# Half rows of a DRAM-to-DRAM shift divided into strips of 10 KB and 6 KB

## The chip, the core and the metric

The kernel runs on one core of one Trainium2 chip. The metric is the device time of one execution in microseconds; the median of the runs before is 821.31 us. The profile and the trace come from one profiled execution, whose times are counted from the start of its span.

## The reference

```python
def setup_inputs():
    return {
        "x": np.random.randn(8192, 8192).astype(np.float32),
    }

def reference(x: np.ndarray) -> np.ndarray:
    return np.fft.ifftshift(x)
```

For even sizes this swaps the quadrants: out[r, c] = x[(r + 4096) % 8192, (c + 4096) % 8192]. Nothing is calculated. A row of 8192 floats is 32 KB, its left and right halves are 16 KB each, and the matrix has 268.44 MB (2^28 bytes), which have to be read once and written once.

## The kernel before, in words

All work is done by DMAs that copy straight from x to out in DRAM; no tile goes through the core. The function `copy` (L26) takes a queue, a row and a column of out, and a list of [step, count] pairs, works out where the same elements lie in x, and issues one DMA at L29. Two queues issue: `nc.sync` (SP; q1 in the profile) copies the left halves of out, `nc.scalar` (ACT; q10) the right halves.

A block is `rows` = 16 x 16 = 256 rows. The DMA of a block's half has the pattern `back`: 16 rows beside each other, 16 steps back by 16 rows each, and in each of them 4096 floats that lie together. The innermost run of 16 KB is one packet of a DMA engine. The outermost count of 16 is dealt to the 16 DMA engines, one row of every 16 to each; an engine then walks backward through the block with a step of 16 rows (512 KB) from packet to packet. One such DMA moves 4 MB.

The loop takes groups of four blocks from the last rows of out to the first, and in each the blocks 3, 2, 1, 0 on SP; on ACT, block (n + 2) % 4 of the same group goes with block n on SP, so that the two queues are two blocks (512 rows) apart.

Ahead of the loop ACT issues seven small copies. They move the last 16 rows of the right half of one block in four strips of 4 KB, three of which are divided by rows into 14 + 2, 9 + 7 and 4 + 12. A DMA whose outermost count is k below 16 uses k engines, so the engines get between one and seven of these 64 pieces. The DMA that moves the rest of this block, with the pattern `rest`, is one step of 16 rows shorter.

In all there are 32 DMAs on SP and 39 on ACT. The framework has eight semaphores for DMAs and gives them out in turn, so that a DMA that gets a semaphore already given has to wait at its issue until the DMA that had it before is done. In steady state four DMAs of each queue are in flight, and each issue waits for the DMA four back on its own queue. Within a DMA engine both queues have a row of packets waiting, and the engine takes from one and the other.

Of the kernel before, what the change touches and what calls it, by code (L numbers as in the profile page):

```python
# [1 line left out]

# [4 lines left out]


ENGINES = 16


@with_exitstack
def kernel(
    ctx: ExitStack,
    tc: tile.TileContext,
    x: bass.AP,
    out: bass.AP,
):
    nc = tc.nc
    R, C = x.shape  # L20
    hr = R // 2
    hc = C // 2
    per = 16
    rows = ENGINES * per

    def copy(queue, row, col, dims):  # L26

        src = (row + hr) % R * C + (col + hc) % C
        queue.dma_start(  # L29
            out=bass.AP(out.tensor, out.offset + row * C + col, dims),  # L30
            in_=bass.AP(x.tensor, x.offset + src, dims),
        )

    start = R - 3 * rows
    strip = hc // 4
    for n, k in enumerate((14, 9, 4)):
        col = hc + n * strip
        copy(nc.scalar, start + rows - ENGINES, col, [[C, k], [1, strip]])  # L40
        copy(nc.scalar, start + rows - ENGINES + k, col, [[C, ENGINES - k], [1, strip]])
    copy(nc.scalar, start + rows - ENGINES, hc + 3 * strip, [[C, ENGINES], [1, strip]])


    back = [[C, ENGINES], [-ENGINES * C, per], [1, hc]]
    rest = [[C, ENGINES], [-ENGINES * C, per - 1], [1, hc]]
    for first in range(R - 4 * rows, -1, -4 * rows):
        for n in (3, 2, 1, 0):
            copy(nc.sync, first + n * rows + rows - ENGINES, 0, back)
            right = first + (n + 2) % 4 * rows  # L50
            if right == start:
                copy(nc.scalar, right + rows - 2 * ENGINES, hc, rest)
            else:
                copy(nc.scalar, right + rows - ENGINES, hc, back)


# [1 line left out]
_INS = ['x']  # L58
_OUTS = [((8192, 8192), 'float32')]


# [23 lines left out]
```

## Time and profile before

| | |
|---|---|
| median of 3 runs | 821.31 us (820.95 to 821.79) |
| span of the profiled execution (its time as a whole is not given beside it) | 810.9 us |
| what the median has over the span | 10.4 us |
| data moved, mean rate over the span | 268.44 MB, 331 GB/s |
| HBM read and written together | 662 GB/s |
| DMA issues of 4 MB: SP / ACT | 32 / 31, and one of 3840 KB on ACT |
| from issue to landing, median and longest | 100.8 us, 104.6 us |
| one DMA instruction on SP | 571 ns |
| last issue on SP / ACT | at 706.2 us / 714.7 us |

How to read it: the engines of the core are all but idle, so the usual rows of busy engines and of the critical chain hold nothing here (the chain is 0.4 us of start-up on POOL). The rows that matter are those of the DMA engines: their busy share and their rate by slice of time, the packets and the share of each queue, and the durations of single packets in the trace. A busy DMA engine is not one at its full pace; a packet that waits for memory counts as busy.

### The profile page before, as it was taken

Reading aid. Unit: us, or ns where it says so; the run is one execution under the profiler, and the core shown is the slowest. Engines: PE = TensorE matmul, PEld = TensorE weight load, DVE = VectorE, ACT = ScalarE, POOL = GpSimd, SP = SyncE. Lnnn points to the kernel's source line nnn. Section 1 sums busy time; section 2 is a strip of 40 time slices with the busy share of each in tenths; the row PEclk is TensorE's granted clock in tenths of the full one; section 3 lists DMA queues with packets and bytes.
Section 4 is the critical chain, followed back from the end, with each engine's and each line's share of the span. In section 5 each row is a group of like instructions: output and inputs, shape, how many; then the busy total and the mean of one; then the engine's idle time right before and its main releaser. Section 6 shows DMA issues by size and latency. Waiting matters only on the chain. (4 is left out here: it accounts for less than half of the span.)

```text
span 810.9 us, 116 instructions
## 1 busy us (share of the span) xinstructions
POOL 0.2 (0%) x4
## 2 busy tenths in 40 slices
POOL 0000000000000000000000000000000000000000
DMA  9999999999999999999999999999999999999998
GB/s 302 328 335 329 334 333 331 331 335 330 326 331 329 331 335 330 332 332 337 335 336 333 333 337 330 334 335 331 336 331 333 335 334 335 333 330 336 333 338 296
DMA packets 17520, 268.44 MB, mean 331 GB/s; under 512 B 1088, under 2 KB 1088, under 8 KB 1152
## 3 DMA queue, kind: packets, MB, share of 16 engines
q1 hardware_dynamic: 8704, 134.22, 49.7%
q10 hardware_dynamic: 8816, 134.22, 49.6%
HBM read 268.44 MB, written 268.44 MB: 662 GB/s over the span
## 5 line engine op out<-in xcount | busy, mean ns | idle before, releaser
L69 POOL MEMSET const-bfloat16-1.0<- 128x1 bf16 x1 | 0.1, 102 | 0.0
L69 POOL MEMSET const-uint8-127<- 128x1 uint8 x1 | 0.1, 102 | 0.0
L69 POOL MEMSET const-float32-0.0<- 128x1 f32 x1 | 0.1, 99 | 0.2 <-issue 0.2
L69 POOL MEMSET const-float32-1.0<- 128x1 f32 x1 | 0.1, 99 | 0.0
## 6 DMA issues: line engine op xcount, KB each, us to landing
out_dram<-in_x_dram SPq DMA_DIRECT2D x32, 4096.0 KB, 100.9
out_dram<-in_x_dram ACTq DMA_DIRECT2D x31, 4096.0 KB
out_dram<-in_x_dram ACTq DMA_DIRECT2D x1, 3840.0 KB
out_dram<-in_x_dram ACTq DMA_DIRECT2D x1, 64.0 KB, 10.8
out_dram<-in_x_dram ACTq DMA_DIRECT2D x1, 56.0 KB
out_dram<-in_x_dram ACTq DMA_DIRECT2D x1, 48.0 KB
out_dram<-in_x_dram ACTq DMA_DIRECT2D x1, 36.0 KB
out_dram<-in_x_dram ACTq DMA_DIRECT2D x1, 28.0 KB
```

The costliest lines, as they stand in the source:

```text
L69: nc = _bacc.Bacc("TRN2", target_bir_lowering=False, num_devices=1)
```

## The change

The special start on ACT goes. A block has 512 rows in place of 256. The half row is divided at column `cut` = 4096 x 5/8 = 2560 floats, 10 KB, which leaves 6 KB. For each of the 16 blocks, from the last to the first, SP copies the 10 KB strip and then the 6 KB strip of the block's left half; ACT copies, of the right half of the block that lies 8 blocks (4096 rows) away, first the 6 KB strip and then the 10 KB one. A DMA has 512 packets as against 256, 32 on each engine; it moves 5 MB or 3 MB. Each queue issues 32 DMAs. The step between engines (one row, 32 KB) and between an engine's packets in one DMA (16 rows, 512 KB) stays.

```diff
-    per = 16
+    per = 32
     rows = ENGINES * per
+    cut = hc * 5 // 8
 
-    def copy(queue, row, col, dims):
-
+    def strip(queue, row, col, width):
         src = (row + hr) % R * C + (col + hc) % C
+        dims = [[C, ENGINES], [-ENGINES * C, per], [1, width]]
         queue.dma_start(
             out=bass.AP(out.tensor, out.offset + row * C + col, dims),
             in_=bass.AP(x.tensor, x.offset + src, dims),
         )
 
-    start = R - 3 * rows
-    strip = hc // 4
-    for n, k in enumerate((14, 9, 4)):
-        col = hc + n * strip
-        copy(nc.scalar, start + rows - ENGINES, col, [[C, k], [1, strip]])
-        copy(nc.scalar, start + rows - ENGINES + k, col, [[C, ENGINES - k], [1, strip]])
-    copy(nc.scalar, start + rows - ENGINES, hc + 3 * strip, [[C, ENGINES], [1, strip]])
-
-    back = [[C, ENGINES], [-ENGINES * C, per], [1, hc]]
-    rest = [[C, ENGINES], [-ENGINES * C, per - 1], [1, hc]]
-    for first in range(R - 4 * rows, -1, -4 * rows):
-        for n in (3, 2, 1, 0):
-            copy(nc.sync, first + n * rows + rows - ENGINES, 0, back)
-            right = first + (n + 2) % 4 * rows
-            if right == start:
-                copy(nc.scalar, right + rows - 2 * ENGINES, hc, rest)
-            else:
-                copy(nc.scalar, right + rows - ENGINES, hc, back)
+    blocks = R // rows
+    for n in reversed(range(blocks)):
+        left = n * rows + rows - ENGINES
+        right = (n + blocks // 2) % blocks * rows + rows - ENGINES
+        strip(nc.sync, left, 0, cut)
+        strip(nc.scalar, right, hc + cut, hc - cut)
+        strip(nc.sync, left, cut, hc - cut)
+        strip(nc.scalar, right, hc, cut)
```

## The prediction

> **What bounds the kernel now.** I read the first page's table of slices and its queue rows, then bandwidth by stretch of time, then what the SP queue waits for, and last the trace's record of every DMA packet (start, duration, size, queue).
>
> ```profile
> span 810.9 us, 116 instructions
> ...
> DMA  9999999999999999999999999999999999999998
> GB/s 302 328 335 329 334 333 331 331 335 330 326 331 329 331 335 330 332 332 337 335 336 333 333 337 330 334 335 331 336 331 333 335 334 335 333 330 336 333 338 296
> DMA packets 17520, 268.44 MB, mean 331 GB/s; under 512 B 1088, under 2 KB 1088, under 8 KB 1152
> ## 3 DMA queue, kind: packets, MB, share of 16 engines
> q1 hardware_dynamic: 8704, 134.22, 49.7%
> q10 hardware_dynamic: 8816, 134.22, 49.6%
> ```
>
> The 16 DMA engines are busy from end to end (a 9 in every slice but the last), no compute engine does anything, and each queue has half the engines' time. So the time is the sum of the packets' durations, and the change acts through what one packet takes. q1 is SP's queue: of its 8704 packets 512 are 4-byte semaphore writes (32 DMAs x 16 engines), so 8192 carry 16 KB. Their mean is 0.497 x 16 x 810.9 us / 8192 = 787 ns; the packet records give 786.5 over both queues.
>
> The same records show that 34% of the 16 KB packets take 608 to 615 ns, and none takes less. I read 611 ns as the engine's own pace and the other 175 ns of the mean as stalls: 175 x 1022 packets per engine = 179 us of the span. This is by far the largest term that the change can touch. Is the stall a contest between the two queues? The stretches say no:
>
> ```profile
> core 0: us, POOL busy (x), PEclk, DMA share, GB/s
> ...
> 2.20:5.00 2.80, 0.00 (x0) 1.00 0.95 351
> ...
> 17.50:23.50 6.00, 0.00 (x0) 1.00 1.00 328
> 24.00:100.00 76.00, 0.00 (x0) 1.00 1.00 331
> 100.00:800.00 700.00, 0.00 (x0) 1.00 1.00 333
> ```
>
> In the first row only q1 has packets, in the second only q10 (8 semaphore writes apart), in the last two both do. One queue alone ran at 328 and 351 GB/s, both together at 331 and 333. So the stall is not made by having two queues at work, and a change that only alters what one queue does beside the other has no clear hold on it.
>
> ```profile
> SPq L29 <- DMA out_dram<-in_x_dram: 686.8, 28, 28.4
> ```
>
> SP waits in 28 of its 32 issues for a DMA of its own that is four back. With three more in flight behind the one waited for, and engines at a share of 1.00, this wait costs nothing now.
>
> **The change, part by part.** The sum is made against the profiled span, 810.9 us. The median of the runs is 821.3 us, so 10.4 us lie around the span; the change touches nothing there and I add them at the end.
>
> Bytes: 268.44 MB before and after. Nothing gained or lost.
>
> Packets: a half row of 16 KB becomes one of 10 KB and one of 6 KB. Data packets go from 8192 + 8176 + 64 = 16,432 to 64 DMAs x 512 = 32,768; 16,336 more, 1021 per engine. Semaphore writes go from 1088 to 1024. The trace has no 10 or 6 KB packet, but the kernel's start moves 64 packets of 4 KB: 53 of them took 156 to 166 ns, median 159. Against 611 ns for 16 KB, 12,288 bytes cost 452 ns, 4096 bytes then 151 ns, and 8 ns remain per packet (a 10 KB one would take 385 ns and a 6 KB one 234 ns, together 619 against 611). Consecutive records on an engine overlap by 4 ns, so the net can be as little as 4 ns. Fully exposed this is 1021 x 8.3 = 8.5 us, or 1021 x 4.3 = 4.4 us by the smaller figure. But an engine that waits for memory anyway can hide it: packets at their own pace fill only 0.34 x 611 / 786 = 26% of the time. Bounds are 1.2 us (26% of 4.4) and 8.5 us; I take a third of the upper, **+2.9 us**, because stalled packets are the greater part. The Trainium skill (DMA: Bandwidth & Descriptors, Why small descriptors are slow) gives a fixed cost of about 3 cycles per packet inside the engine. At the 850 MHz of the same page that would be an estimated 3.6 us for 1021 packets; the trace agrees with the size (4 to 8 ns a packet).
>
> Stalls, per byte or per packet: the 4 KB packets' mean is 185 ns, so they stalled for 26 ns; the 16 KB ones for 175. A straight line through both has 12 ns per KB and nothing left at zero bytes (-24 ns). So stalls go with bytes in this trace, and cutting packets leaves them at 175 ns per 16 KB. The sample is small and from the first 15 us alone, so I keep the other end: if all of the 26 ns went with each new packet, 1021 x 26 = 27 us more. I take **0**, by the line. The pattern of addresses could also lower the stall, which is the first rival.
>
> The start on ACT: the seven small copies go. Their 64 pieces are unevenly dealt: by their 14, 2, 9, 7, 4, 12 and 16 rows, engine 0 gets seven and engine 15 one, four on average. If the fullest engine ends last, three pieces of 159 to 185 ns, 0.5 us, leave the end: **-0.5 us**. If not, 0. ACT alone fills the engines for some 6 us at 328 GB/s because SP's second DMA has to wait until its first is done, and this gap in SP's work goes as well: 6 x (333 - 328) / 328 = 0.1 us, nothing. The small copies also set how far ACT trails SP; what is late next is ACT's first packet, which came 2.8 us after SP's (the first of the stretches above) and has no reason to come earlier.
>
> Waits on issue: 64 DMAs take the place of 71, each queue still issuing 32 and waiting for its own fourth one back, now for 5 MB and 3 MB DMAs in turn. Behind the waiting instruction are only later DMAs of the same queue. At worst 3 + 5 + 3 MB are in flight on that queue, 69 us of work at its half of 333 GB/s, against about 1.5 us from an issue at 0.7 us to the first packets at 2.2 us. The cover holds: **0**. If it went, the other queue's packets would still fill the engines, as the stretch with q10 alone shows.
>
> Sum: 810.9 + 2.9 - 0.5 = 813.3 us of span, with 10.4 around it **823.7, say 824 us**, 0.3% slower. The runs before spread over 0.1%, so 0.2% is about the least that a measurement of this kernel can tell from no change.
>
> **The rivals.**
>
> *Stalls ease (not slower).* The place is the memory wait inside the packets. Both queues now never work on the same part of a half row: SP is in columns 0 to 10 KB of its half row while ACT is in 10 to 16 KB of its own. If stalls come from streams standing at the same position of 16 KB, this spreads them. For it: the stall term is 179 us, and the slices' GB/s move between 326 and 338 though the work per byte is the same, so addresses do matter. Against it: one queue alone, with all engines in the same columns, was no slower (351 and 328). Price: the best slice kept all along, 800 us x (1 - 333/338) = -11.8, with the +2.4 of above 801.5 + 10.4 = 812 us. The far end is the 351 GB/s of a stretch of 2.8 us: 800 x (1 - 333/351) = -41, or 783 us. It decides early: the 2.4 us of the sum are 2.3 ns of the 175 per 16 KB, so stalls shorter by 1.3% cancel them, and by 2.3% make the kernel faster by 0.2%. I give weight to the slices, since they last 20 us. The Trainium skill (the same page, Latency and other measured facts) reports that copies with row pitches of large powers of two lose much rate and that a 4 KB pad restores it. Were the 16 KB spacing of the two queues here such a pitch, the change would act like a pad; no run so far shows it, and the pitches inside each queue (32 KB and 512 KB) stay.
>
> *Stalls come with each new packet (slower).* The place is the engine's step from one packet to the next, in another half row and now 1021 times more on each engine. It leaves my forecast's range, 829 us, where a new packet stalls for over 5 ns on top of the 2.9 us. Price: up to 27 + 8.5 us, 857 us; the slowest inner slice, 326 GB/s kept all along, gives 800 x (333/326 - 1) = 17.2, with the +2.4 841 us. I use 841. For it: smaller pieces change rows twice as often. Against it: the straight line above.
>
> *The strips don't stay paired (the change doesn't do what it says).* Nothing but equal packet counts holds 10 KB beside 6 KB. SP has 2.8 us before ACT's first packet, which at 385 ns is 7 packets of the 32 in a DMA; over those both queues carry the same width, about a fifth of the time. If the lag were near 32 they never pair. Since the rate was the same with one queue or two, I expect 824 +- 3 us in this case.
>
> **How the numbers follow.** Forecast (stalls unchanged, 821 to 829): 0.38. Stalls ease (797 to 819): 0.34. Stalls per packet (829 to 857): 0.20. Strips unpaired (821 to 827): 0.08. Faster by over 0.2% (below 819.7) is the second case with a little of the first, 0.35. Within 0.2% (up to 822.9) is the lower part of the first and last, 0.14; slower is the rest, 0.51. The range leaves out a tenth at each end: 805 to 843 us. The cases of both signs hold most of the chance, so the likeliest one's own range is 821 to 829 us.
>
> **What would show it.** Packets should number 33,792, of which 1024 are under 2 KB and 17,408 under 8 KB. The smallest durations of a 10 and a 6 KB packet should be near 385 and 234 ns, and the sum of their means 786 + 3 = 789 ns. Inner slices should stay at 326 to 338 GB/s with 332 in the middle. A sum of means near 775 means that stalls ease; one above 800 that packets bring stalls of their own. The wait for SP's own DMAs should stay long and without effect, at a DMA share of 1.00. I am wrong if that share falls below 0.98 in mid run (descriptors come too slowly), or if the rate of the inner slices moves by over 1%: then the addresses decide, and not the count of packets.

## The result and the profile after

The changed kernel takes 841.35 us (median of 4 runs, 839.93 to 842.49) beside 821.13 us for the kernel before: 1.023 times, with an interval of 1.0211 to 1.025. That is 20 us slower where 3 were forecast.

The page of the kernel after, with the rows that were shown of before:

```profile
span 838.1 us, 109 instructions
...
DMA  8999999999999999999999999999999999999997
GB/s 293 328 326 317 322 319 317 329 326 322 328 318 320 325 326 324 326 326 321 318 326 323 324 319 323 322 325 323 316 325 329 319 325 324 316 327 317 326 321 252
DMA packets 33792, 268.44 MB, mean 320 GB/s; under 512 B 1024, under 2 KB 1024, under 8 KB 17408
...
q1 hardware_dynamic: 16896, 134.22, 49.5%
q10 hardware_dynamic: 16896, 134.22, 49.4%
```

The data are the same, the packets 33,792 as worked out, and the DMA engines are again busy to the end. But the inner slices now lie at 316 to 329 GB/s where they were at 326 to 338, and the last one is at 252 where it was at 296: the rate in mid run fell, and the end frays out. The wait of SP, now at line 32, is shorter and still without effect, since the DMA share in the slices stays at nine tenths or more:

```profile
SPq L32 <- DMA out_dram<-in_x_dram: 228.4, 28, 25.0
```

One figure of the prediction falls at once. The page of after belongs to an execution of 839.93 us, and its span is 838.1: 1.8 us lie around a span, not 10.4. By that the first profile of before was of an execution of some 813 us, 1% faster than its listed runs. So of the fall of the rate from 333 to 323 GB/s between 100 and 800 us, about a third belongs to the execution that was profiled and not to the change. The kernel before varies by that much from one set of runs to another: it took 820.8 us beside the first four experiments, 810.7 beside the next four and 811.9 beside the last four. The record gives the chips of these sets the numbers 2, 4 and 2, so it isn't shown that the chip makes the difference. In what follows each kernel is given as a ratio to before in its own set, and durations of packets are compared only within a set.

The packet records of after: the fastest 10 KB and 6 KB packets take 382 to 385 and 232 to 234 ns, as forecast. The sum of the means of the two is 809 ns against the forecast 789.

### The profile page after: what moved, and what is told of

Same layout as the page of the kernel before. It is cut to its first block, busy times and chain, and to the rows that moved or that the text cites. A ratio compares the mean times of both kernels' runs of the same rounds, so it can differ in the third digit from the quotient of the medians.

```text
span 838.1 us, 109 instructions
## 1 busy us (share of the span) xinstructions
POOL 0.2 (0%) x4
## 2 busy tenths in 40 slices
DMA packets 33792, 268.44 MB, mean 320 GB/s; under 512 B 1024, under 2 KB 1024, under 8 KB 17408
```

## The experiments

Four explanations stood. A: each added packet costs some 20 ns. B: the frame costs, that is the lost start on ACT, the 512-row blocks and the distance of 8 blocks. C: widths that differ between the queues at the same moment cost. D, formed after the first four: lengths that are no multiple of 4 KB cost. A fifth, F, was formed after eight runs and is told in its place.

**Whole half rows in the frame of after**

```diff
-        strip(nc.sync, left, 0, cut)
-        strip(nc.scalar, right, hc + cut, hc - cut)
-        strip(nc.sync, left, cut, hc - cut)
-        strip(nc.scalar, right, hc, cut)
+        strip(nc.sync, left, 0, hc)
+        strip(nc.scalar, right, hc, hc)
```

> The frame of after (no small copies at the start, 512 rows to a block, 8 blocks between the queues) with whole half rows of 16 KB. Theory A, each added packet costs (20 us for 1021 more packets on each engine, 20 ns each): as few packets as before, so 821 +- 3 us. Theory B, the frame costs (lost start, other distance between the queues): stays at 841 +- 4 us. Theory C, the unequal widths of the two queues cost: 821 as in A.

Measured: 1.0023 (1.0004 to 1.0041). The frame with its lost start costs 0.2%, and 0.4% at the most by the interval; B falls.

**The strips in the frame of before**

```diff
-            copy(nc.sync, first + n * rows + rows - ENGINES, 0, back)
...
+            strip(nc.sync, left, 0, per, cut)
+            strip(nc.scalar, right, hc + cut, steps, hc - cut)
+            strip(nc.sync, left, cut, per, hc - cut)
+            strip(nc.scalar, right, hc, steps, cut)
```

Here `strip` calls `copy` with the pattern of a strip; `steps` is 16, or 15 for the block whose last 16 rows the small copies move.

> The frame of before (its small copies at the start, 256 rows to a block, the queues two blocks apart) with its half rows divided at 10 KB and changed over as in after. Theory A (packets): 841 +- 4 us, sum of the means of a 10 KB and a 6 KB packet 800 to 815 ns. Theory B (frame): 821 to 825 us. Theory C (unequal widths): 841.

Measured: 1.0244 (1.0225 to 1.0264). The strips alone bring the whole loss; the start doesn't protect from it. The sum of means was 804 ns, and the last slice of the page 188 GB/s.

**The cut in the middle**

```diff
-    cut = hc * 5 // 8
+    cut = hc * 4 // 8
```

> After with the cut at 8 KB, so that both queues move equal strips; as many packets as after. Theory A (packets): 841 +- 4 us, two 8 KB packets together 805 to 812 ns, each at least 310 ns. Theory B (frame): 841. Theory C (unequal widths): 821 plus only the fixed cost of 8.5 us, so 826 to 831 us.

Measured: 1.0028 (1.0016 to 1.0041). This is the surprise. As many packets as in after, all DMAs in the same order, and the loss is all but gone. Its page:

```profile
DMA  8999999999999999999999999999999999999998
GB/s 301 328 327 332 329 329 330 331 330 317 328 331 331 329 326 328 329 328 331 326 322 330 330 326 330 324 327 332 330 324 328 333 331 329 329 326 329 328 327 294
DMA packets 33792, 268.44 MB, mean 327 GB/s; under 512 B 1024, under 2 KB 1024, under 8 KB 1024
```

The packet count is that of after, the inner slices are at 317 to 333 and the last one is at 294, as in before. Two 8 KB packets took 794 ns together, while one 16 KB packet took 797 in the whole half rows above, in the same set: the fixed 8 ns more were paid out of shorter stalls (176 against 186 ns per 16 KB). A falls: doubling the packets, from 16 KB to 8 KB, is almost free.

**Four strips of 4 KB**

```diff
-    cut = hc * 5 // 8
+    cut = hc // 4
...
-        strip(nc.sync, left, 0, cut)
-        strip(nc.scalar, right, hc + cut, hc - cut)
-        strip(nc.sync, left, cut, hc - cut)
-        strip(nc.scalar, right, hc, cut)
+        for k in range(4):
+            strip(nc.sync, left, k * cut, cut)
+            strip(nc.scalar, right, hc + (k + 2) % 4 * cut, cut)
```

> After's frame with four strips of 4 KB to a half row: 3 x 1021 more packets on each engine than before. Theory A with 20 ns per packet: 821 + 61 = 882 +- 8 us. If only the engine's fixed 8 ns per packet grows and the stalls stay as in after: 841 + 2 x 8.5 = 858 us. Theory B (frame): 841 to 845. Theory C (unequal widths): 821 + 3 x 8.5 = 847 us.

Measured: 1.0322 (1.0302 to 1.0342), 847.7 us. It met the number of C (847), but its page shows that not all of it is a cost per packet:

```profile
GB/s 276 318 317 319 326 318 322 321 323 321 319 322 321 319 321 318 326 322 324 316 324 320 322 322 325 321 324 320 323 326 314 325 325 325 324 322 325 324 325 182
DMA packets 67584, 268.44 MB, mean 317 GB/s; under 512 B 2048, under 2 KB 2048, under 8 KB 67584
```

The last slice has only 182 GB/s. The engines were idle for 10.3 us each, on average, in the last 20 us of the data, against 0.8 us with the even cut. So in this kernel the engines end far apart, with strips that are all equal.

**Before again, for a profile beside the next three.** 

> The kernel before, unchanged, for a profile of it on the same chip as the three others. The first profile of it has a span of 810.9 us beside runs of 821 us; the later kernels' profiled executions are only 1.8 us longer than their spans. If that first execution was a fast one, this span should be 817 to 821 us, the mean 16 KB packet 792 to 797 ns, and the 16 engines should again finish each DMA within 1 to 3 us of each other.

Measured: 0.9997 (0.9976 to 1.0018), span 808.3 us. The mean 16 KB packet took 783 ns, less than expected, as the kernel before was faster in this set (810.7 us); the engines finished a DMA within about 2 us of each other. Stretches of this run, to hold against the next kernel:

```profile
core 0: us, POOL busy (x), PEclk, DMA share, GB/s
24.00:100.00 76.00, 0.00 (x0) 1.00 0.99 333
100.00:400.00 300.00, 0.00 (x0) 1.00 1.00 333
430.00:700.00 270.00, 0.00 (x0) 1.00 1.00 334
...
790.00:800.00 10.00, 0.00 (x0) 1.00 0.99 334
800.00:810.00 10.00, 0.00 (x0) 1.00 0.60 200
```

**Both queues in step: 10 KB beside 10 KB, then 6 beside 6**

```diff
         strip(nc.sync, left, 0, cut)
-        strip(nc.scalar, right, hc + cut, hc - cut)
+        strip(nc.scalar, right, hc, cut)
         strip(nc.sync, left, cut, hc - cut)
-        strip(nc.scalar, right, hc, cut)
+        strip(nc.scalar, right, hc + cut, hc - cut)
```

> After with the two queues in step: both move 10 KB strips, then both 6 KB strips; same packets, same sizes. Theory C (widths that differ between the queues at the same moment): 824 +- 4 us, and the engines finish a DMA within 3 us of each other. Theory D (lengths and starts that are no multiple of 4 KB): 841 +- 4 us. Theory A (number of packets): excluded by the even cut, would be 841.

Measured: 1.0271 (1.0236 to 1.0306). Theory C expected the loss to go, and it did not, though ACT's trail of some five packets of 32 still puts unlike widths together for about a sixth of the time. The same stretches:

```profile
core 0: us, POOL busy (x), PEclk, DMA share, GB/s
24.00:100.00 76.00, 0.00 (x0) 1.00 1.00 326
100.00:400.00 300.00, 0.00 (x0) 1.00 1.00 329
430.00:700.00 270.00, 0.00 (x0) 1.00 1.00 328
...
790.00:800.00 10.00, 0.00 (x0) 1.00 1.00 339
800.00:810.00 10.00, 0.00 (x0) 1.00 0.80 303
810.00:820.00 10.00, 0.00 (x0) 1.00 0.57 241
820.00:830.00 10.00, 0.00 (x0) 1.00 0.24 101
```

Where before is done at 807 us, this kernel runs out slowly: the DMA share goes 0.80, 0.57, 0.24 over the last 30 us. The first engine was done some 31 us ahead of the last. The loss is 24 us, and two parts of like size make it up: the engines idled 13.1 us each in the last 20 us of data, 12.2 more than before did (0.9), and 328 to 329 GB/s in place of 333 to 334 over 800 us are about 12 more. Counted over the last 40 us the idle time is 15.7 us, so the two parts are known to some 3 us only.

**The cut at 12 KB, and at 9 KB**

```diff
-    cut = hc * 5 // 8
+    cut = hc * 3 // 4
```

and in the other kernel

```diff
-    cut = hc * 5 // 8
+    cut = hc * 9 // 16
```

> After with the cut at 12 KB: 12 KB and 4 KB strips. Theory C (unequal at the same moment): more unequal, so 841 to 855 us, with engines 6 us or more apart at a DMA's end. Theory D (no multiple of 4 KB): 824 +- 4 us.

> After with the cut at 9 KB: 9 KB and 7 KB strips. Theory C, if the cost grows with the difference of the widths: 2 KB of difference in place of 4, so 828 to 836 us. Theory C, if any inequality is enough: 841. Theory D (no multiple of 4 KB, here not even of 2 KB): 841 or more.

Measured: 1.0207 (1.017 to 1.0244) for 12 + 4 KB and 1.0075 (1.0047 to 1.0103) for 9 + 7 KB. D falls twice: the lengths that are multiples of 4 KB are slow, and those that are not even a multiple of 2 KB are the least slow of the unequal cuts. C is not borne out by 12 + 4 KB: it expected 841 us or more beside 821 (1.024), and 1.0207 lies below that, though its interval just reaches it. The 9 KB cut, at about the lower end of what C named (828 us beside 821, 1.0085), doesn't speak against C.

**What these eight have in common.** Each engine ends its part of a DMA with a semaphore write, which the packet records hold. The time from the first to the last of the 16 writes says how far the engines are apart. Where that time comes near the time between two DMAs, the writes of one DMA mix with those of the next, and they have to be sorted by the semaphore that they go to; this is so in the three kernels marked with a star. For SP's DMAs, in us, mid run being 100 to 800 us:

| kernel | first DMA | median in mid run | last DMA | time, ratio to before |
|---|---|---|---|---|
| before (first profile) | 3.0 | 1.6 | 2.0 | 1 |
| whole half rows | 1.2 | 2.4 | 2.5 | 1.0023 |
| cut at 8 KB | 0.9 | 1.1 | 1.3 | 1.0028 |
| cut at 9 KB | 1.1 | 2.4 | 3.2 | 1.0075 |
| cut at 12 KB | 4.9 | 10.7 | 10.0 | 1.0207 |
| after (10 KB) | 3.4 | 6.7 | 8.1 | 1.023 |
| strips in the frame of before * | 1.7 | 18.7 | 17.3 | 1.0244 |
| both queues in step * | 1.1 | 22.4 | 31.6 | 1.0271 |
| four strips of 4 KB * | 3.1 | 22.2 | 20.6 | 1.0322 |

Kernels whose engines stay within 2.5 us to the end are within 0.3% of before, and all whose engines drift to 6 us and more are slower by 2% or more, with the 9 KB cut between. That is theory F: the cost is that the engines fall out of step. But the loss doesn't simply grow with the distance: 6.7 us in after cost no less than 10.7 with the cut at 12 KB, and a row of numbers is no proof. One kernel even speaks against F as the cause of the lower rate in mid run. With both queues in step the distance grows all along, from some 1 us at the first DMA to 4 at 106 us, 22 at 453 us and 40 at 788 us, yet the rate is 326 GB/s from 24 to 100 us, where before had 333, and 328 to 329 later. So there the rate was low before the engines were far apart, and didn't fall further as they drifted; the distance shows in the end of the run alone. The last four runs were chosen to part F from C and from G, the changing over (each queue moves from one width to the other at every DMA).

**After again, beside the next three.** 

> After, unchanged, for its time and profile on the same chip as the three others. Theory F (the drift: with unequal lengths the engines fall apart and end apart) and theory C (unequal widths stall more) both expect 1.023 times the time of before, engines 6 to 9 us apart at the late DMAs.

Measured: 1.0167 (1.0144 to 1.019), less than the 1.023 of the first result, with intervals that don't overlap. The engines were a little less far apart here (6.0 us in mid run against 6.7). Why the two sets differ stays open.

**No changing over**

```diff
     for n in reversed(range(blocks)):
...
         strip(nc.sync, left, 0, cut)
         strip(nc.scalar, right, hc + cut, hc - cut)
+    for n in reversed(range(blocks)):
...
         strip(nc.sync, left, cut, hc - cut)
         strip(nc.scalar, right, hc, cut)
```

> After without the changing over at every DMA: SP moves all its 10 KB strips and then all its 6 KB strips, ACT the other way round, so the widths differ at every moment but near the middle. Theory C (unequal at the same moment stalls): 1.020 to 1.030 of before, rate 318 to 323 GB/s or less in mid run. Theory G (the changing over itself does it, because ACT trails by five packets and the two queues then move like widths): 1.003 to 1.010.

Measured: 1.0134 (1.0104 to 1.0163), between the two expectations, and not clearly apart from after's 1.0167. The engines are 4 us apart on SP's DMAs and 8 on ACT's in mid run. The changing over is not the main cause; whether it adds some tenths of a per cent can't be told from this.

**Even cut, both queues on the same part**

```diff
-    cut = hc * 5 // 8
+    cut = hc * 4 // 8
...
         strip(nc.sync, left, 0, cut)
-        strip(nc.scalar, right, hc + cut, hc - cut)
+        strip(nc.scalar, right, hc, cut)
         strip(nc.sync, left, cut, hc - cut)
-        strip(nc.scalar, right, hc, cut)
+        strip(nc.scalar, right, hc + cut, hc - cut)
```

> The even cut at 8 KB, but both queues on the same part of their half rows (0 to 8 KB together, then 8 to 16 KB). Theory of the first rival (streams at the same position of 16 KB stall): slower than the even cut with the queues on opposite parts (1.003 of before), so 1.01 or more. If the position of the queues against each other has no effect: 1.000 to 1.006.

Measured: 1.0028 (1.0005 to 1.0051), the same as with the queues on opposite parts. Where the two queues stand against each other in the half row has no effect that these runs can see. Its engines stay 1.1 us apart.

**10 KB for half of the blocks, then 8 KB**

```diff
-    cut = hc * 5 // 8
...
     for n in reversed(range(blocks)):
+        cut = hc * 5 // 8 if n >= blocks // 2 else hc * 4 // 8
```

> After for the first eight blocks, then the even cut at 8 KB for the last eight. Theory C: 320 to 323 GB/s up to 410 us and 327 to 330 after 430 us, time 1.011 to 1.016 of before. Theory F: the engines are 4 to 5 us apart at DMAs' ends in the first half; if equal lengths bring them together again, under 2 us in the second and no loss at the end; if equal lengths only keep them as they are, still 4 us apart at the end and the last slice as low as in after (252 GB/s against 294).

Measured: 1.0179 (1.0144 to 1.0213), no better than after. This run decides on C. Stretches of three kernels of the same set; the last column is GB/s. First the even cut with both queues on the same part:

```profile
core 0: us, POOL busy (x), PEclk, DMA share, GB/s
...
100.00:400.00 300.00, 0.00 (x0) 1.00 0.99 332
430.00:700.00 270.00, 0.00 (x0) 1.00 0.99 332
```

Then after:

```profile
core 0: us, POOL busy (x), PEclk, DMA share, GB/s
...
100.00:400.00 300.00, 0.00 (x0) 1.00 1.00 328
430.00:700.00 270.00, 0.00 (x0) 1.00 1.00 328
```

Then this kernel, whose change of strips falls at about 410 us:

```profile
core 0: us, POOL busy (x), PEclk, DMA share, GB/s
...
100.00:400.00 300.00, 0.00 (x0) 1.00 1.00 328
430.00:700.00 270.00, 0.00 (x0) 1.00 0.99 326
```

In the second stretch this kernel runs even 8 KB strips, the very DMAs, in the same order, that the kernel with the cut at 8 KB runs there, and it gets 326 GB/s. Even strips give 332 in the first of the three, whose queues stand otherwise, which by the two ratios of 1.0028 changes nothing. In stalls, after the change of strips this kernel has 179 ns per 16 KB and the even cut 165; 14 ns over 1024 half rows per engine would be 14 us in a whole run. So C, by which the second half should have been fast, falls, and with it every explanation by which the lengths of the strips that are being moved are all that sets the rate. In the second half the rate is low because of something that the unequal strips left behind. The end is in between: the last of the page's 40 slices has 275 GB/s, where after has 259 and the even cut 303.

Two such things are in the packet records. The engines are 5.6 us apart when the even strips begin, and still 5.4 at the last DMA; even strips don't bring them together. That is F. But the queues' distance stays as well: ACT is 5.3 packets behind SP here, as in after, and 6.3 in both even cuts. Is it that trail (theory H)? The 9 KB cut has a trail of 5.35 and the paired kernel 5.34, in one set with before again (333 to 334 GB/s). The first holds 330 to 331 GB/s with its engines 2.4 us apart, the second 328 to 329 while the distance grows to 40 us, and the cut at 12 KB, with a trail of 4.4 and 11 us, 326. One trail, two rates: it doesn't explain the whole. And without the changing over ACT is 120 packets ahead of SP from 430 to 700 us, and the rate is 329 GB/s there as it was from 100 to 400 us. H isn't excluded for a part, though. Even strips with the trail shifted by one packet would have told this; that wasn't tried.

## Why the prediction was right and wrong

**The time is the sum of the packets' durations.** Right for most of the run: after's DMA share is 1.00 from 100 to 800 us, so no wait for an issue took part. At the end it left out that engines which are done early stand idle; see below.

**Packets, +2.9 us.** The size per packet was right (382 to 385 and 232 to 234 ns at the engine's own pace). The cover may have been better than the third that I took, which was a choice and not a measurement: whole half rows and halves of 8 KB, both in one set and in one frame, stand at 1.0023 and 1.0028. The estimate of 3.6 us for 1021 packets, worked out from the 3 cycles a packet of the Trainium skill (DMA: Bandwidth & Descriptors, Why small descriptors are slow), finds no support: the difference of the two ratios, 0.05% or 0.4 us, is smaller, though their intervals allow some 3 us, and so hardly rule out the 2.9.

**Stalls, 0 by the straight line.** This is the step that failed: stalls went with something else than bytes. The kernel after and the even cut of the same set (the last four runs) have 797.0 and 782.1 ns per 16 KB; of that 619 and 618 are the engine's own pace, which leaves 178 and 164 ns of stall. The 14.9 ns of difference are 15 us of the run. The bytes are the same in both, so a stall that goes with bytes alone can't give it. The straight line rested on 64 packets of 4 KB and on packets of one kernel only, and could not show what another division of the rows would do. What sets the stall stays open.

**The end, -0.5 us for the start on ACT.** Wrong in sign for the end as a whole. Engines that are 6 to 7 us apart end apart: 3.2 us of idle time per engine in the last 20 us of data in after, 0.7 in the even cut of the same set, so +2.5 us. Stall and end together are 17.8 us, and the gaps between packets, less the small overlaps of the records, are some 4.5 us shorter in after, which leaves 13.3. The data of the two kernels take 821.1 and 807.9 us from the first packet to the last: 13.2. This is an account of where the time lies, and doesn't show a cause. What leaving out the small copies did by itself was not measured apart.

**The waits on issue, 0, and the frame.** Right within 0.4%: the whole half rows in the new frame are at 1.0023 (1.0004 to 1.0041).

**The rivals.** *Stalls ease* did not happen, and its mechanism is not there: on opposite parts or on the same part of the half row, the even cut stands at 1.0028. The Trainium skill (DMA: Bandwidth & Descriptors, Latency and other measured facts) reports that a 4 KB pad of a large row pitch restores the rate of copies; no run here changed the row pitch, so none shows it. *Stalls with each new packet* named 841 us and 841.35 came, but for another reason: that the price fitted was luck and the mechanism was wrong, as twice the packets in even strips cost 0.3% together with the new frame. Its sign came too, a sum of means above 800 ns (809), and so did the sign that addresses decide, a rate in mid run that moves by over 1%; the even cut refutes the first reading, and no run bears out the second. *The strips don't stay paired* was right about the trail (ACT is some five packets behind SP all along) and right that pairing doesn't matter: in step, opposed or never changing over, the unequal cut is slow.

So the direction was right and the size was not, 20 us in place of 3. The time lies far above the 821 to 829 us of the likeliest case and just inside the wide range of 805 to 843 us, which reached so far because of that rival. The cause was in no part of the prediction.

**What is settled and what stays open.** Shown: the strips alone bring the loss (in either frame). It is not that there are two to a half row, not the position of one queue's strip beside the other's, not that the widths differ between the queues at one moment, and not lengths off a multiple of 4 KB. Engines that drift apart end apart, which is about half of the loss in the paired kernel and 2.5 us in after; the lower rate in mid run outlasts the unequal strips. Not settled: where that lower rate, the larger part of the loss in after, comes from. How far the engines are out of step doesn't set it in the paired kernel, and the trail between the queues doesn't set it without the changing over; either may have a part elsewhere. Nor is it known why unequal strips let the engines drift and half rows or halves of 8 KB don't, and why 4 KB strips, though equal, drift as well.

None of these kernels beats the one before; the nearest are at 1.0023 and 1.0028.

## What to carry to other kernels

When a copy has every DMA engine busy, look at how far the engines are apart at each DMA's end before counting packets: here that went with the loss from kernel to kernel, though it is shown as a cause for the end of the run only, and the number of packets from 16 KB to 8 KB did not. A cut into equal pieces of 8 KB was all but free, while 9 + 7, 10 + 6 and 12 + 4 KB cost 0.8 to 2.3%. A straight line fitted to the packets of one kernel did not hold for another, and a profile that is 1% off the median of the runs must be set against its own execution first.

## What the runs showed of the hardware

- Sixteen engines with equal work stayed within 1 to 2.5 us of each other over 800 us, although each queue lets them run up to four DMAs (some 100 us) apart, or they drifted up to 40 us apart (both queues in step); once apart by 5.6 us they stayed so for 400 us of even strips.
- The same kernel took 820.8 us in one set of runs and 810.7 in another, on chips of the numbers 2 and 4, but 811.9 in a later set under number 2; 1.8 us lay around the span in the first two (824.1 and 822.3 us of the whole half rows; 810.1 and 808.3 of before).
- Going from 16 KB packets to twice as many of 8 KB lowered the stalls by 10 ns per 16 KB (186 to 176), which paid for the added 8 ns.
